# Hand-overs between layers: where the first paired weight tile is summed and split, and when the third plain tile is split

## The chip, the cores and the metric

The kernel runs on one core of a Trainium2 chip. Time is device time in microseconds (us) for one execution, median of three. A profile of one more execution gives the rows shown below. Engine names are those of the profile: PE (TensorE, matrix products; PEld its weight loads), DVE (VectorE), ACT (ScalarE), POOL (GpSimd), SP (SyncE, which here only issues DMAs).

## The reference

Two layers on 512 tokens of width 1024. Each layer is: FFN, mixer, FFN, each one between two RMS norms and added to the residual `h`.

```python
for layer in range(DEPTH):
    g = norm_g[layer]
    f = swiglu_ffn(rms_norm(h, g[0]), ffn_w_gate[layer, 0], ffn_w_up[layer, 0], ffn_w_down[layer, 0])
    h = h + 0.5 * rms_norm(f, g[1])
    hn = rms_norm(h, g[2])
    # layer 0: m = pooling and state-space mixer of hn; layer 1: m = neighbourhood attention of hn
    h = h + rms_norm(m, g[3])
    f = swiglu_ffn(rms_norm(h, g[4]), ffn_w_gate[layer, 1], ffn_w_up[layer, 1], ffn_w_down[layer, 1])
    h = h + 0.5 * rms_norm(f, g[5])
```

`swiglu_ffn` is `(silu(x @ w_gate) * (x @ w_up)) @ w_down` with inner width 2816, so 22 column tiles of 128.

## The kernel before

**Precision.** Every fp32 matrix product is made of three fp32r products: both operands are split into a part `hi` and a rest `lo`, and `mm3` (L170 to L172) adds hi·hi, lo·hi and hi·lo. So each weight tile has to be split before PE can use it: `Weights.hi` copies it on ACT (L113, tile `w_hi`), `Weights.lo` subtracts on DVE or POOL (L124, tile `w_lo`). Activations are transposed on PE (L297) into PSUM (`ps_t`) and evacuated from there in two steps: `xT_hi` on ACT (L318) and `xT_lo` on DVE (L319).

**Paired weight tiles.** An FFN multiplies some column tiles plainly (14 in the first FFN, 2 in the others; gate and up each, so 4 plain weight tiles at the start of the others) and the rest in pairs, by seven products of sums in place of eight. For a pair two raw tiles are loaded, `w_raw` and `w_u`. `Weights.sums` (L95, L96, L98) forms their sums, and the four tiles g, s, u, h that follow are split like plain ones. The sums of the activation blocks are made once for each FFN by `x_sums`: t1, t2, t3, then t4, each split into `xsum..._0` (ACT, L485) and `xsum..._1` (DVE, L488). `x_sums` is a generator; the FFN takes a step of it after each of the four plain tiles of token pair 1.

**A hand-over** is the stretch from the last products of one block to the first of the next. There are five: first FFN to mixer (order "mix"), mixer to FFN, FFN to FFN across the layers, and attention to FFN (order "nat", three of them), and FFN to attention (order "att"). `finish_rows` runs it: products of token tiles 0 and 1, then 2, then 3 (`ps_B`); beside the last of them `residual` adds the normed result to `h` for pair 0, `h_sumsq` (ACT, tile `junk`) and `pre_norm` make `xn`, and `pending()` is `to_xT`: 16 transposes, then 8 evacuations. `first_proj` of the next block multiplies the first four weight tiles with pair 0 (96 products of 256 columns), calls the second `pending()` for pair 1, and multiplies the same four tiles with pair 1.

**What sets the order.** All instructions are issued in the order of the code, to each engine's own queue; an engine waits at its front instruction. On ACT the third next weight tile's `hi` stands ahead of the last sum of squares over `ps_B` and of all evacuations of pair 0:

```python
        W.hi()
        W.hi()
        fg()
        fg = self.post_tile(3, 1, psB, True)
        fg()
        W.lo(nc.gpsimd)
        W.load_ahead()
        W.lo(nc.gpsimd)
        W.load_ahead()
        pending()
```

At most two raw tiles are held at a time, so a load is issued when a `lo` has read an older one. `w_u`, `w_s` lie in the pool `fast`, which `start()` allocates at the beginning of the FFN, after the second `pending()`.

Of the kernel before, what the change touches and what calls it, by code (L numbers as in the profile page):

```python
# [12 lines left out]
ALU = mybir.AluOpType  # L13
# [149 lines left out]
class Builder:  # L163
# [234 lines left out]
        sl = slice(t * P, (t + 1) * P)  # L398
        self.mm3(ps, [x[:, sl] for x in lhs(kt)], [x[:, j * HALF:(j + 1) * HALF] for x in w], start, stop)

    def finish_rows(self, cp, psB, tail, kts, lhs, opened, nxt):


        nc = self.nc
        self.W.fill(self.W.n_split)
        n = 2 * len(tail)

        def product(i, t):
            w = tail[i // 2]
            self.rows(psB[t], lhs, kts[i], t, w, i % 2, not opened and i == 0, i == n - 1)  # L410

        def finish(ts, parts=1):
            for t, sl in self.residual(ts, parts):
                if nxt is None:
                    nc.sync.dma_start(self.out[t * P:(t + 1) * P, sl], self.h[:, t, sl])
            if nxt is not None:
                return self.h_sumsq(cp, ts[0] // 2)

        for i in range(n):
            for t in (0, 1):  # L420
                product(i, t)
        self.post_pair(0, 1, psB)
        s = finish((0, 1))
        for i in range(n):
            product(i, 2)
        fg = self.post_tile(2, 1, psB, True)
        if nxt is None:
            fg()
            finish((2,))
        for i in range(n):  # L430
            product(i, 3)
            if i % 2:
                self.W.done(fill=False)
        if nxt is None:
            self.post_tile(3, 1, psB)
            return finish((3,), 2)

        W = self.W
        W.hi()
        pending = self.pre_norm(cp, 0, s, nxt[0], nxt[1])  # L440
        W.lo()
        W.load_ahead()
        W.hi()
        W.hi()
        fg()
        fg = self.post_tile(3, 1, psB, True)
        fg()
        W.lo(nc.gpsimd)
        W.load_ahead()
        W.lo(nc.gpsimd)  # L450
        W.load_ahead()
        pending()
        return self.pre_norm(cp, 1, finish((2, 3)), nxt[0], nxt[1])


    b_order = list(range(NF))
# [10 lines left out]
    def x_sums(self, forms, tmp, gain=None):  # L467

        nc, tt, W = self.nc, self.nc.vector.tensor_tensor, self.W
        f32 = lambda k, n: [x.bitcast(F32) for x in self.x_block(k, n)]
        b12, b22, t2, t3, t1 = tmp

        def second(out, k):
            if gain is None:
                tt(out=out, in0=f32(k, 1)[0], in1=f32(k, 1)[1], op=ALU.add)
                return
            for kt in range(4 * k, 4 * k + 4):  # L480
                nc.scalar.activation(out=out[:, kt % 4], in_=self.ps_t[kt // 2][:, kt % 2 * 256:(kt % 2 + 1) * 256],
                                     func=AF.Copy, scale=self.gcol[:, gain * KT + kt:gain * KT + kt + 1])

        def hi(n, x):
            nc.scalar.copy(forms[n][0], x)  # L485

        def lo(n, x):
            tt(out=forms[n][1], in0=x, in1=forms[n][0].bitcast(F32), op=ALU.subtract)  # L488

        W.load_ahead()  # L490
        second(b12, 0)
        W.hi()
        second(b22, 1)
        W.sums(W.tiles[W.split][1], nc.vector)
        tt(out=t1, in0=b12, in1=f32(0, 0)[0], op=ALU.subtract)
        tt(out=t1, in0=t1, in1=f32(0, 0)[1], op=ALU.subtract)
        tt(out=t2, in0=t1, in1=b22, op=ALU.subtract)
        tt(out=t3, in0=b22, in1=b12, op=ALU.subtract)
        W.lo()
        W.load_ahead()  # L500
        yield
        W.hi()
        hi(2, t2)
        hi(3, t3)
        hi(1, t1)
        lo(2, t2)
        W.lo()
        lo(3, t3)
        lo(1, t1)
        yield  # L510
        W.hi()
        W.lo()
        t4 = b12
        tt(out=t4, in0=t2, in1=f32(1, 0)[0], op=ALU.add)
        tt(out=t4, in0=t4, in1=f32(1, 0)[1], op=ALU.add)
        yield
        hi(4, t4)
        W.hi()
        lo(4, t4)
        W.lo()  # L520
        W.load_ahead()
        yield
# [5 lines left out]
    def ffn(self, layer, which, gain, nxt, before, ssm=None):  # L528
# [5 lines left out]
        tc, nc, V = self.tc, self.nc, self.nc.vector  # L534
# [4 lines left out]
        def start():  # L539

            z["up"] = tc.alloc_tile_pool(name="up", bufs=1)
            self.W.fast = tc.alloc_tile_pool(name="fast", bufs=1)
            z["t"] = t_pool = tc.alloc_tile_pool(name="xsum", bufs=1, side="right", reuse_waits="tile")
            z["forms"] = forms = {n: [t_pool.tile([P, 4, 256], F32R, name="xsum%d_%d" % (n, i)) for i in range(2)]
                                  for n in (2, 3, 1, 4)}
            tmp = [z["g"][1][:, NF - 6 + 2 * i:NF - 4 + 2 * i].rearrange("p a (b c) -> p (a b) c", c=256)
                   for i in range(3)]
            tmp += [z["up"].tile([P, 1024], F32, tag="m", bufs=2, name="m").rearrange("p (a c) -> p a c", c=256)
                    for _ in range(2)]
            z["sums"] = self.x_sums(forms, tmp, None if ssm else gain)  # L550
            next(z["sums"], None)

        def finish(f, ps_g, ps_u):
            g = z["g"][1][:, f]
            nc.scalar.activation(out=g, in_=ps_g, func=AF.Silu)
            V.tensor_tensor(out=g, in0=g, in1=ps_u, op=ALU.mult)
# [44 lines left out]
        def last_sums(f, up, m, m34):  # L601
            V.tensor_tensor(out=m[:, 256:768], in0=m[:, 256:768], in1=m34, op=ALU.add)  # L602
            if up:
                nc.gpsimd.tensor_tensor(out=rows(f), in0=rows(f), in1=m, op=ALU.mult)  # L604
            else:
                nc.scalar.activation(out=rows(f), in_=m, func=AF.Silu)

        for f in range(n_plain, NF, 2):
            for up in range(2):
# [24 lines left out]
                self.W.done(fill=not last)  # L634
                if not last:
                    last_sums(f, up, m, m34)
        self.W.fast.release()
        self.W.fast = None
        t_pool.release()
        if ssm:  # L640
            self.new_psum(("ps_A", "ps_t"), ("ps_B", "ps_m", "ps_k", "ps_p"))
            self.xT_pool.release()
# [1 line left out]
        r_pools = {n: tc.alloc_tile_pool(name="gT%d" % n, bufs=1, side="right", reuse_waits="tile")  # L644
                   for n in ((8, 2) if ssm else (2, 8))}
        parts, ahead = {}, []
# [12 lines left out]
        order = self.b_order  # L659
# [14 lines left out]
        if ssm:  # L674
            free_pool = tc.alloc_tile_pool(name="free", bufs=1, side="right", reuse_waits="tile")
            free = [free_pool.tile([P, n], F32, name="free%d" % i) for i, n in enumerate((4608, 4608, 2048))]
# [16 lines left out]
        psB = [self.bank("ps_B") for _ in range(TT)]  # L693
        n_out = NF - NTAIL
        tail = []
# [18 lines left out]
        cp = tc.alloc_tile_pool(name="chain", bufs=1)  # L714
        self.chain_begin(cp, 0.5)
        for pair in range(2):
            self.post_pair(pair, 0, psA)
        pending = self.finish_rows(cp, psB, tail, order[n_out:], parts.get, True, nxt)
        return pending, lambda: [p.release() for p in (cp, *list(r_pools.values())[::-1])]

# [1071 lines left out]
```

## Time and profile before

| what | value |
|---|---|
| median of three runs | 1927.48 us (1927.22 to 1929.05) |
| the profiled execution | 1925.91 us, its span 1924.1 us |
| PE busy | 1847.0 us, 96% of the span |
| DVE busy | 1471.0 us, 76% |
| ACT busy | 924.7 us, 48% |
| POOL busy | 349.2 us, 18% |

The span goes from the first to the last instruction; 1.8 us of the profiled execution lie outside it. Busy shares are means over very different stages. Times in rows are counted from the start of the span.

### The profile page before, as it was taken

Reading aid. Unit: us, or ns where it says so; the run is one execution under the profiler, and the core shown is the slowest. Engines: PE = TensorE matmul, PEld = TensorE weight load, DVE = VectorE, ACT = ScalarE, POOL = GpSimd, SP = SyncE. Lnnn points to the kernel's source line nnn. Section 1 sums busy time; section 2 is a strip of 40 time slices with the busy share of each in tenths; the row PEclk is TensorE's granted clock in tenths of the full one; section 3 lists DMA queues with packets and bytes.
Section 4 is the critical chain, followed back from the end, with each engine's and each line's share of the span. In section 5 each row is a group of like instructions: output and inputs, shape, how many; then the busy total and the mean of one; then the engine's idle time right before and its main releaser. Section 6 shows DMA issues by size and latency. Waiting matters only on the chain.

```text
span 1924.1 us, 31539 instructions
## 1 busy us (share of the span) xinstructions
PE 1847.0 (96%) x12368; PEld 1653.5 (86%) x12368; DVE 1471.0 (76%) x2380; ACT 924.7 (48%) x1749; POOL 349.2 (18%) x238
## 2 busy tenths in 40 slices
PE   7999998998899999999899999989999999999998
PEld 7877986887679999988899998879878789999886
DVE  6788979968769999844799996455565569999744
ACT  5244446454455444534545445346555455445432
POOL 1021221014001223100022320001222001332100
PEclk9999999999999999999999999999999999999999
DMA  5464346537422333322233223213222122323321
GB/s 192 144 210 153 110 139 197 194 117 253 157 88 99 108 101 104 116 100 75 78 110 110 99 88 132 99 66 117 93 99 99 66 89 88 111 99 110 114 95 66
DMA packets 82021, 225.48 MB, mean 117 GB/s; under 512 B 15792, under 2 KB 20048, under 8 KB 80848
## 3 DMA queue, kind: packets, MB, share of 16 engines
q1 hardware_dynamic: 70176, 197.80, 30.2%
q0 software_dynamic: 6960, 23.57, 4.1%
q10 hardware_dynamic: 4736, 2.10, 0.4%
q8 instruction: 97, 1.59, 0.3%
q14 instruction: 52, 0.43, 0.1%
HBM read 206.69 MB, written 18.84 MB: 117 GB/s over the span
## 4 chain that ended last, share of the span: by engine, by line
PE 63%; DVE 7%; ACT 2%; DMA 1%; issue 1%; DVEq 0%; ACTq 0%
PE ps_gu L172 10%; PE ps_gu L171 10%; PE ps_gu L170 10%; PE ps_A L172 3%; PE ps_A L171 3%; PE ps_A L170 3%; PE ps_B L172 3%; PE ps_B L171 3%; PE ps_B L170 3%; PE ps_f L170 3%; PE ps_f L171 2%; PE ps_f L172 2%; DVE w_lo L124 1%; PE ps_p L171 1%; PE ps_p L172 1%
## 5 line engine op out<-in xcount | busy, mean ns | idle before, releaser
L124 DVE TENSOR_TENSOR w_lo<-w_raw,w_hi 128x1024 fp32r<-128x1024 f32 x214 | 282.9, 1327 | 212.0 <-ACT w_hi L113 211.9
L113 ACT CAST w_hi<-w_raw 128x1024 fp32r<-128x1024 f32 (+1 forms) x313 | 262.8, 864 | 276.0 <-PE ps_A L172 72.4
L170 PE MATMUL ps_gu<-xsum,w_hi 128*128 128x256 f32 x1088 | 309.0, 284 | 5.7 <-ACT xsum L485 5.7
L171 PE MATMUL ps_gu<-xsum,w_hi 128*128 128x256 f32 x1088 | 309.5, 284 | 2.8 <-DVE xsum L488 2.6
L172 PE MATMUL ps_gu<-xT_hi,w_lo 128*128 128x256 f32 (+1 forms) x1008 | 308.6, 306 | 2.7 <-DVE w_lo L124 2.7
L172 PE MATMUL ps_gu<-xsum,w_lo 128*128 128x256 f32 x1088 | 309.1, 284 | 0.0
L170 PE MATMUL ps_gu<-xT_hi,w_hi 128*128 128x256 f32 (+1 forms) x1008 | 306.6, 304 | 0.0
L171 PE MATMUL ps_gu<-xT_lo,w_hi 128*128 128x256 f32 (+1 forms) x1008 | 306.2, 304 | 0.0
L170 PEld LDWEIGHTS ps_gu<-xsum,w_hi 128*128 128x128 f32 x1088 | 209.3, 192 | 6.3 <-ACT xsum L485 6.3
L171 PEld LDWEIGHTS ps_gu<-xsum,w_hi 128*128 128x128 f32 x1088 | 209.5, 193 | 3.6 <-DVE xsum L488 3.6
L172 PEld LDWEIGHTS ps_gu<-xsum,w_lo 128*128 128x128 f32 x1088 | 209.8, 193 | 0.0
L172 PEld LDWEIGHTS ps_gu<-xT_hi,w_lo 128*128 128x128 f32 x1008 | 191.6, 190 | 14.7 <-DVE w_lo L124 3.7
L170 PEld LDWEIGHTS ps_gu<-xT_hi,w_hi 128*128 128x128 f32 x1008 | 191.7, 190 | 9.0 <-issue 0.7
L171 PEld LDWEIGHTS ps_gu<-xT_lo,w_hi 128*128 128x128 f32 x1008 | 191.4, 190 | 7.5
L98 POOL TENSOR_TENSOR w_u<-w_raw,w_s 128x512 f32<-128x512 f32 x64 | 111.5, 1743 | 381.3 <-ACT w_hi L113 196.1
L124 POOL TENSOR_TENSOR w_lo<-w_raw,w_hi 128x1024 fp32r<-128x1024 f32 x31 | 73.7, 2380 | 569.2 <-ACT w_hi L113 500.6
L113 ACT CAST w_hi<-w_s 128x512 fp32r<-128x512 f32 x136 | 77.7, 621 | 193.7 <-DVE w_s L96 191.6
L96 DVE TENSOR_TENSOR w_s<-w_raw,w_u 128x1024 f32<-128x1024 f32 x68 | 145.8, 2145 | 2.4
L170 PE MATMUL ps_p<-xT_hi,w_hi 128*128 128x256 f32 (+1 forms) x416 | 127.2, 306 | 20.0 <-ACT xT_hi L318 19.7
L172 PE MATMUL ps_A<-w_hi,gT 128*128 128x512 f32 x352 | 138.5, 394 | 6.9 <-DVE gT L657 6.9
L604 POOL TENSOR_TENSOR g<-g,m 128x1024 f32<-128x1024 f32 x34 | 94.6, 2781 | 245.4 <-DVE m L602 239.1
L170 PE MATMUL ps_A<-w_hi,gT 128*128 128x512 f32 x352 | 138.1, 392 | 0.0
(376 smaller groups left out, 4286.2 us busy)
## 6 DMA issues: line engine op xcount, KB each, us to landing
w_raw<-in_w_gu_dram SPq DMA_DIRECT2D x106, 512.0 KB, 3.3
w_raw<-in_w_dn_dram SPq DMA_DIRECT2D x88, 512.0 KB, 3.2
w_u<-in_w_gu_dram SPq DMA_DIRECT2D x70, 512.0 KB, 3.7
w_raw<-in_w_qk_dram SPq DMA_DIRECT2D x16, 512.0 KB, 3.3
bias<-in_att_bias_dram SPq DMA_DIRECT2D x16, 512.0 KB, 4.1
w_raw<-in_w_in_dram SPq DMA_DIRECT2D x8, 512.0 KB, 3.2
cm<-m_dram SPq DMA_DIRECT2D x4, 1024.0 KB, 8.3
w_raw<-in_w_ao_dram SPq DMA_DIRECT2D x8, 512.0 KB, 4.0
```

Source lines behind the costliest of these rows:

```text
L96: tt(out=blocks(s), in0=g[:, :HALF].unsqueeze(1).broadcast_to([P, 2, HALF]), in1=blocks(u)[:, :2], op=ALU.subtract)
L98: (h_engine or self.nc.gpsimd).tensor_tensor(out=u[:, :HALF], in0=g[:, HALF:], in1=s[:, HALF:], op=ALU.add)
L113: self.nc.scalar.copy(hi[:, k:k + step], src[:, k:k + step])
L124: (engine or self.lo_engine).tensor_tensor(out=lo[:, :n], in0=src, in1=hi[:, :n].bitcast(F32), op=ALU.subtract)
L170: mm(ps, a[0], b[0], start=start, stop=False)
L171: mm(ps, a[0], b[1], start=False, stop=False)
L172: mm(ps, a[1], b[0], start=False, stop=stop)
L604: nc.gpsimd.tensor_tensor(out=rows(f), in0=rows(f), in1=m, op=ALU.mult)
```

## The change

Three things are rearranged; no operation is added or taken away.

1. In all five hand-overs the third next plain tile's `hi` and `lo` move from ahead of `pending()` into it, behind the first four of its eight evacuations (`between`).
2. In the three "nat" hand-overs the pool `fast` is allocated in `finish_rows`, on the right side of the memory instead of the left, so that the first `w_u` is loaded there. `hi` of the first paired tile (g) follows the first `pending()`; its `sums` and its `lo` follow `pre_norm` of pair 1, so they stand on DVE ahead of the evacuations of pair 1. In `x_sums` these steps are left out (`gain is None` only for the first FFN).
3. In `x_sums` t4 is computed one step earlier, ahead of the split of t1.

To make room, the pools of the down-projection's input (`gT`) are released inside `finish_rows`, after the last products.

```diff
+        free()
         if nxt is None:
             self.post_tile(3, 1, psB)
             return finish((3,), 2)
...
         W.lo()
         W.load_ahead()
         W.hi()
-        W.hi()
         fg()
         fg = self.post_tile(3, 1, psB, True)
         fg()
         W.lo(nc.gpsimd)
         W.load_ahead()
-        W.lo(nc.gpsimd)
-        W.load_ahead()
-        pending()
-        return self.pre_norm(cp, 1, finish((2, 3)), nxt[0], nxt[1])
+
+        def between():
+            W.hi()
+            W.lo(nc.gpsimd)
+            W.load_ahead()
+
+        ahead = nxt[1] == "nat"
+        if ahead:
+            W.fast = self.tc.alloc_tile_pool(name="fast", bufs=1, side="right")
+            W.load_ahead()
+        pending(between)
+        if ahead:
+            W.hi()
+        pending = self.pre_norm(cp, 1, finish((2, 3)), nxt[0], nxt[1])
+        if ahead:
+            W.sums(W.tiles[W.split][1], nc.vector)
+            W.lo()
+            W.load_ahead()
+        return pending
...
         second(b12, 0)
-        W.hi()
+        if gain is None:
+            W.hi()
         second(b22, 1)
-        W.sums(W.tiles[W.split][1], nc.vector)
+        if gain is None:
+            W.sums(W.tiles[W.split][1], nc.vector)
...
-        W.lo()
-        W.load_ahead()
+        if gain is None:
+            W.lo()
+            W.load_ahead()
         yield
...
         lo(3, t3)
+        t4 = b12
+        tt(out=t4, in0=t2, in1=f32(1, 0)[0], op=ALU.add)
+        tt(out=t4, in0=t4, in1=f32(1, 0)[1], op=ALU.add)
         lo(1, t1)
         yield
         W.hi()
         W.lo()
-        t4 = b12
-        tt(out=t4, in0=t2, in1=f32(1, 0)[0], op=ALU.add)
-        tt(out=t4, in0=t4, in1=f32(1, 0)[1], op=ALU.add)
```

ACT at the hand-over from the mixer to its FFN, before, from `xn` of pair 0 on. `junk,ss_5281` is the last sum of squares over `ps_B`, `junk,ss_h` those of pair 1, and the rows `g<-ps_t` are blocks that `x_sums` reads.

```order
L286 ACTIVATE xn<-h,rs_r 128x512 x2
L113 CAST w_hi<-w_raw 128x1024 x2
L226 ACTIVATE junk,ss_5281<-ps_B 128x512
L318 ACTIVATE xT_hi<-ps_t,gcol 128x256 x8
L226 ACTIVATE junk,ss_h<-h 128x1024 x2
L286 ACTIVATE xn<-h,rs_r 128x512 x2
L318 ACTIVATE xT_hi<-ps_t,gcol 128x256 x8
L481 ACTIVATE g<-ps_t,gcol 128x256 x4
L113 CAST w_hi<-w_raw 128x512 x2
L481 ACTIVATE g<-ps_t,gcol 128x256 x4
L113 CAST w_hi<-w_s 128x512 x2
```

The same place on ACT in the changed kernel:

```order
L286 ACTIVATE xn<-h,rs_r 128x512 x2
L113 CAST w_hi<-w_raw 128x1024
L226 ACTIVATE junk,ss_5281<-ps_B 128x512
L318 ACTIVATE xT_hi<-ps_t,gcol 128x256 x4
L113 CAST w_hi<-w_raw 128x1024
L318 ACTIVATE xT_hi<-ps_t,gcol 128x256 x4
L113 CAST w_hi<-w_raw 128x512 x2
L226 ACTIVATE junk,ss_h<-h 128x1024 x2
L286 ACTIVATE xn<-h,rs_r 128x512 x2
L318 ACTIVATE xT_hi<-ps_t,gcol 128x256 x8
L498 ACTIVATE g<-ps_t,gcol 128x256 x8
L113 CAST w_hi<-w_s 128x512 x2
```

One `w_hi` of 1024 columns has moved behind four evacuations, and the two halves of the paired tile's `w_hi` ahead of the sums of squares of pair 1.

DVE at the same hand-over, before, from `xn` of pair 1 on; L95, L96 and L98 are the weight sums, L495 to L498 give t1, t2 and t3.

```order
L287 TENSOR_SCALAR xn<-h,rs_r 128x512 x2
L319 SCALAR_TENSOR_TENSOR xT_lo<-ps_t,gcol,xT_hi 128x256 x8
L95 TENSOR_TENSOR w_u<-w_u 128x512
L96 TENSOR_TENSOR w_s<-w_raw,w_u 128x1024
L98 TENSOR_TENSOR w_u<-w_raw,w_s 128x512
L495 TENSOR_TENSOR m<-g,xT_hi 128x1024
L496 TENSOR_TENSOR m<-m,xT_lo 128x1024
L497 TENSOR_TENSOR g<-m,g 128x1024
L498 TENSOR_TENSOR m<-g 128x1024
L124 TENSOR_TENSOR w_lo<-w_raw,w_hi 128x1024
L488 TENSOR_TENSOR xsum_1_5585<-g,xsum_0_5584 128x1024
L124 TENSOR_TENSOR w_lo<-w_s,w_hi 128x1024
```

The same place on DVE in the changed kernel:

```order
L287 TENSOR_SCALAR xn<-h,rs_r 128x512 x2
L95 TENSOR_TENSOR w_u<-w_u 128x512
L96 TENSOR_TENSOR w_s<-w_raw,w_u 128x1024
L98 TENSOR_TENSOR w_u<-w_raw,w_s 128x512
L124 TENSOR_TENSOR w_lo<-w_raw,w_hi 128x1024
L319 SCALAR_TENSOR_TENSOR xT_lo<-ps_t,gcol,xT_hi 128x256 x8
L514 TENSOR_TENSOR m<-g,xT_hi 128x1024
L515 TENSOR_TENSOR m<-m,xT_lo 128x1024
L516 TENSOR_TENSOR g<-m,g 128x1024
L517 TENSOR_TENSOR m<-g 128x1024
L505 TENSOR_TENSOR xsum_1_5602<-g,xsum_0_5601 128x1024
L124 TENSOR_TENSOR w_lo<-w_s,w_hi 128x1024
```

Four DVE instructions, the three sums and the split of g, stand between `xn` and the evacuations of pair 1 now.

SP's queue at this hand-over, before; `gpost` is the gain of the next norm, `w_raw` and `w_u` the raw tiles.

```order
L74 DMA w_raw<-in_w_gu_dram 128x1024 x5
L222 DMA gpost<-in_norm_g_dram 128x1024
L71 DMA w_u<-in_w_gu_dram 128x2x512
L74 DMA w_raw<-in_w_gu_dram 128x1024
L71 DMA w_u<-in_w_gu_dram 128x2x512
L74 DMA w_raw<-in_w_gu_dram 128x1024
```

And in the changed kernel:

```order
L74 DMA w_raw<-in_w_gu_dram 128x1024 x5
L71 DMA w_u<-in_w_gu_dram 128x2x512
L74 DMA w_raw<-in_w_gu_dram 128x1024
L71 DMA w_u<-in_w_gu_dram 128x2x512
L74 DMA w_raw<-in_w_gu_dram 128x1024
L222 DMA gpost<-in_norm_g_dram 128x1024
```

Two `w_u` and two `w_raw` loads stand ahead of `gpost` now; before, the first `w_u` also had to wait for the transposes of pair 1, whose input lay in its place.

## Rows read from the trace of the kernel before

**Rows 1.** Waits of PE, whole span: us in total, times, longest us.
```profile
PE ps_p L170 <- ACT xT_hi L318: 19.7, 6, 5.0
...
PE ps_gu L170 <- ACT xsum L485: 5.7, 3, 2.0
```

**Rows 2.** Timeline of ACT, mixer to FFN: start us, us, then the instruction.
```profile
560.18 1.04 ACT L113 CAST w_hi<-w_raw 128x1024 fp32r<-128x1024 f32 x1 [2.96 <-DMA w_raw<-in_w_gu_dram]
561.13 0.59 ACT L226 ACTIVATE junk<-ps_B 128x512 bf16<-128x512 f32 x1
...
561.71 0.83 ACT L318 ACTIVATE xT_hi<-ps_t,gcol 128x256 fp32r<-128x256 f32 x2
562.96 1.60 ACT L318 ACTIVATE xT_hi<-ps_t,gcol 128x256 fp32r<-128x256 f32 x4 [0.42 <-DVE xT_lo L319]
```

**Rows 3.** Timeline of PE, mixer to FFN.
```profile
556.98 1.91 PE L297 MATMUL ps_t<-ident,xn 128*128 128x128 f32 x16
...
589.55 0.28 PE L170 MATMUL ps_gu<-xT_hi,w_hi 128*128 128x256 f32 x1
...
604.88 0.28 PE L170 MATMUL ps_gu<-xT_hi,w_hi 128*128 128x256 f32 x1
```

**Rows 4.** Timeline of DVE, mixer to FFN.
```profile
573.52 0.89 DVE L287 TENSOR_SCALAR xn<-h,rs_r 128x512 f32<-128x512 f32 x2
576.89 2.73 DVE L319 SCALAR_TENSOR_TENSOR xT_lo<-ps_t,gcol,xT_hi 128x256 fp32r<-128x256 f32 x6 [2.48 <-ACT xT_hi L318]
...
581.54 0.69 DVE L95 TENSOR_TENSOR w_u<-w_u 128x512 f32<-128x512 f32 x1 [0.90 <-DMA w_u<-in_w_gu_dram]
...
584.14 1.22 DVE L495 TENSOR_TENSOR m<-g,xT_hi 128x1024 f32<-128x1024 f32 x1
...
589.00 1.22 DVE L124 TENSOR_TENSOR w_lo<-w_raw,w_hi 128x1024 fp32r<-128x1024 f32 x1
```

**Rows 5.** Windows: us, PE busy (instructions), granted PE clock, DMA share, GB/s.
```profile
563.00:565.00 2.00, 2.00 (x9) 0.50 0.66 233
565.00:567.00 2.00, 2.00 (x15) 0.71 0.11 37
...
575.00:577.00 2.00, 2.00 (x20) 1.00 0.00 0
...
600.00:602.00 2.00, 1.26 (x6) 0.58 0.00 0
```

**Rows 6.** Timelines of DVE and PE, FFN to FFN.
```profile
933.36 0.88 DVE L287 TENSOR_SCALAR xn<-h,rs_r 128x512 f32<-128x512 f32 x2
937.60 2.73 DVE L319 SCALAR_TENSOR_TENSOR xT_lo<-ps_t,gcol,xT_hi 128x256 fp32r<-128x256 f32 x6 [3.35 <-ACT xT_hi L318]
...
950.27 0.28 PE L170 MATMUL ps_gu<-xT_hi,w_hi 128*128 128x256 f32 x1
...
953.11 0.28 PE L170 MATMUL ps_gu<-xsum,w_hi 128*128 128x256 f32 x1
...
963.29 0.28 PE L170 MATMUL ps_gu<-xT_hi,w_hi 128*128 128x256 f32 x1
```

**Rows 7.** Timelines of DVE and PE, attention to FFN.
```profile
1571.89 0.88 DVE L287 TENSOR_SCALAR xn<-h,rs_r 128x512 f32<-128x512 f32 x2
1576.04 3.75 DVE L319 SCALAR_TENSOR_TENSOR xT_lo<-ps_t,gcol,xT_hi 128x256 fp32r<-128x256 f32 x8 [3.27 <-ACT xT_hi L318]
...
1604.64 0.28 PE L170 MATMUL ps_gu<-xT_hi,w_hi 128*128 128x256 f32 x1
```

**Rows 8.** Timeline of ACT, FFN to mixer, then FFN to attention.
```profile
415.68 1.34 ACT L286 ACTIVATE xn<-h,rs_r 128x512 f32<-128x512 f32 x2 [1.89 <-DVE rs_r L217]
418.80 2.66 ACT L318 ACTIVATE xT_hi<-ps_t,gcol 128x256 fp32r<-128x256 f32 x6 [1.79 <-PE ps_t L297]
...
1294.39 1.34 ACT L286 ACTIVATE xn<-h,rs_r 128x512 f32<-128x512 f32 x2 [1.88 <-DVE rs_r L217]
1298.59 2.67 ACT L318 ACTIVATE xT_hi<-ps_t,gcol 128x256 fp32r<-128x256 f32 x6 [2.85 <-PE ps_t L297]
```

More of the change, by code (lines that the diff above doesn't have):

```diff
@@ L399, in rows, with finish_rows @@
         self.mm3(ps, [x[:, sl] for x in lhs(kt)], [x[:, j * HALF:(j + 1) * HALF] for x in w], start, stop)
-    def finish_rows(self, cp, psB, tail, kts, lhs, opened, nxt):
+    def finish_rows(self, cp, psB, tail, kts, lhs, opened, nxt, free=lambda: None):
         nc = self.nc
@@ L541, in start @@
             z["up"] = tc.alloc_tile_pool(name="up", bufs=1)
-            self.W.fast = tc.alloc_tile_pool(name="fast", bufs=1)
+            if ssm:
+                self.W.fast = tc.alloc_tile_pool(name="fast", bufs=1)
             z["t"] = t_pool = tc.alloc_tile_pool(name="xsum", bufs=1, side="right", reuse_waits="tile")
@@ L636, in ffn @@
                     last_sums(f, up, m, m34)
+        t_pool.release()
         self.W.fast.release()
         self.W.fast = None
-        t_pool.release()
         if ssm:
@@ L717, in ffn @@
             self.post_pair(pair, 0, psA)
-        pending = self.finish_rows(cp, psB, tail, order[n_out:], parts.get, True, nxt)
-        return pending, lambda: [p.release() for p in (cp, *list(r_pools.values())[::-1])]
+        pending = self.finish_rows(cp, psB, tail, order[n_out:], parts.get, True, nxt,
+                                   lambda: [p.release() for p in list(r_pools.values())[::-1]])
+        return pending, cp.release
     KEY0 = (0, 64, 192, 320)
```

## The prediction

> **What bounds the kernel now.** PE is busy for 1847.0 of 1924.1 us, so I read first what it waits for. The list of PE's waits has two lines that belong to the hand-overs [rows 1]: 19.7 us behind `xT_hi` of ACT, in six places of up to 5.0 us, and 5.7 us behind the activation sums `xsum`, in three places of up to 2.0 us. Next I read one hand-over, mixer to FFN, engine by engine. On ACT the third plain tile's `w_hi` stands 2.96 us idle for its DMA, runs from 560.18, and only then come the last `junk` (0.59 us) and the evacuations, the first at 561.71 [rows 2]. PE had begun the 16 transposes at 556.98 and needs 1.91 us for them [rows 3], so from 558.89 until about 562.5 it has nothing: the evacuations are held up by a weight tile that they don't need. The windows show a second loss: with PE busy again the granted clock is 0.50 from 563 to 565 and 0.71 from 565 to 567, the lower level (1.2 GHz) for most of that time [rows 5]. Half of 2 us and 0.29 of 2 us make 1.6 us of lost work for one such fall. On DVE pair 1's `xn` comes at 573.52, its first `xT_lo` (called S below) at 576.89 and then, after a wait of 0.90 us for `w_u`, the paired tile's sums and the activation sums [rows 4]. PE ends pair 1 at 589.55 = S + 12.66 and the seven products of the pair at 604.88 = S + 27.99 [rows 3]; in FFN to FFN these are 950.27 and 963.29, S + 12.67 and S + 25.69 [rows 6], and attention to FFN ends at S + 28.60 [rows 7]. The pair is 84 products. At full speed 24 of them take 953.11 - 950.27 = 2.84 us [rows 6], 0.1183 each, so 84 take 9.94; the rest, 3.1 to 6.0 us, is waiting and a slow clock behind it (0.58 from 600 to 602 [rows 5]).
>
> **Part 1, the third `w_hi` behind four evacuations.** Its DMA still lands at 560.18, so it still ends at about 561.2, and its `lo` on POOL is not later than before. What changes is what follows it on ACT. Before: `junk`, two evacuations (561.71 to 562.96, with 0.42 idle), two more (half of 1.60), and so the fifth at 561.13 + 0.58 + 1.25 + 0.80 = 563.76 [rows 2]. After: the fifth at 561.13. `junk` and four evacuations fit in the idle 2.96 us: they are 2.63 us with their own idle. The eighth evacuation, and with it pair 1's residual, its sums of squares and `xn`, which follow each other on DVE and ACT without PE, come **2.63 us** earlier in each of the five hand-overs. The first gap of PE shrinks from 3.6 us to some tenths, and with it goes the cause of the fall at 563. PE then does its 96 products of pair 0 in 11.36 us and is ready before `xn` is.
>
> What that is worth depends on what PE waits for next, pair 1's transposes and first evacuation. In the mixer and attention orders nothing new stands in between. The first evacuation comes after half of `xn` (0.67 of 1.34 us), four transposes (a quarter of 1.91, 0.48) and the way between engines, which no row isolates. It is bounded by 0 and by the 0.42 of ACT's idle behind a DVE evacuation [rows 2]; I take 0.30, nearer the row. Sum 1.45 behind `xn`. Before, it came at 418.80 with `xn` at 415.68, and at 1298.59 with `xn` at 1294.39, because PE was late (ACT waits 1.79 and 2.85 for the transposes) [rows 8]. After: 415.68 - 2.63 + 1.45 = 414.50 and 1294.39 - 2.63 + 1.45 = 1293.21. **Gains 4.30 and 5.38.** Work behind it is the same and PE is its limit, so they stay.
>
> **Part 2, the paired tile's work beside the second transposes.** In the three nat hand-overs DVE now has, between `xn` and the first `xT_lo`, its three sums (581.54 to 584.14, 2.60) and one `w_lo` (1.22) [rows 4]. With 0.89 of `xn` ahead, S comes at 573.52 - 2.63 + 0.89 + 2.60 + 1.22 = 575.60, against 576.89: 1.29 earlier. FFN to FFN: 933.36 + 2.08 = 935.44 against 937.60 [rows 6], 2.16 earlier; attention to FFN: 1571.89 + 2.08 = 1573.97 against 1576.04 [rows 7], 2.07 earlier. So most of what part 1 brings here goes into a **new wait**: transposes start with the end of `xn`, at about 571.8, end at 573.7, and PE stands until 576.1 for the first `xT_lo`, 2.4 us. ACT's evacuations of pair 1 stand behind the same DVE, as each waits for the one before to be taken over. What the sums need must be there: `w_u` is now loaded to a place of its own, which waits for no transposes of pair 1 and can be issued when the third plain tile's raw data land, at 560.18; ACT's whole wait for such a tile is 2.96 us [rows 2], so I put its landing at about 563, some 9 us ahead of DVE. The paired raw tile is loaded when POOL has read an older one, which no row times; it too has until pair 1's sums of squares, and its `w_hi` needs 1.04 us [rows 2] on ACT, which has nothing else between the eighth evacuation and those sums. The DMA of `gpost`, now behind four weight loads on SP, is used a norm later; it costs nothing.
>
> In return DVE is free behind the evacuations. From S it needs 8 `xT_lo` (3.75 [rows 7]), four activation sums (4 x 1.22), then in turn split t2, `lo` of s, split t3, two operations of t4, split t1, `lo` of u, split t4 and `lo` of h (each 1.22): t4 is split at S + 18.4 and h at S + 19.6. PE gets to the pair at S + 12.67 and to its last twelve products, those of t4 and h, six forms of 1.42 us later, at S + 21.2. Nothing waits, so the pair ends at S + 12.67 + 9.94 = S + 22.61. **Gains behind S: 27.99 - 22.61 = 5.38, 25.69 - 22.61 = 3.08, 28.60 - 22.61 = 5.99.** If that cover of 1.6 to 2.8 us is gone, each us of DVE or ACT beyond it is lost again.
>
> **Part 3, t4 a step earlier.** It is part of the DVE order just counted. In the first FFN it stands alone; t4 comes up to one split (1.22) sooner. Between 0 and 1.2; no row here shows that PE waits there, so 0.
>
> **The sum.** Mixer and attention orders 4.30 + 5.38 = 9.68. Nat: 1.29 + 5.38 = 6.67, 2.16 + 3.08 = 5.24, 2.07 + 5.99 = 8.06, together 19.97. In all 29.65 of 1925.91. Against it stands the unknown cost of the new waits: PE waits about a us for `xn`, works 1.9 us on transposes, waits 2.4 us. Does the clock fall there? Waits of 3.6 brought a fall [rows 5], and those behind `xsum` of at most 2.0 [rows 1] brought one at 600 [rows 5]; transposes and products without a wait at 575 to 577 kept 1.00 [rows 5]. So 0 to 1.6 in each of three places, 0 to 4.8. The rows are on both sides, and I take half, 2.4. That leaves 27.25: 1898.7 for an execution like the profiled one. The median of the three is 1.57 above that execution, so **1900.2 us**.
>
> The Trainium skill speaks against the change here: "TensorE: Matmul & The Clock Gate", section "HAM oscillation — how this bites in real kernels", says that pauses of PE between bursts of products put the clock back, so that each burst starts slow. By it each new wait would cost a fall, the gain would be 24.85 (29.65 - 4.8) and not 27.25; by the row at 575 alone, 29.65. The row at 600 agrees with the page for a short wait, but no row here shows a wait, transposes and a wait in turn.
>
> **The rivals.** *The new DVE work eats the gain of nat.* If all three falls happen and pairs still wait behind ACT's splits, say half of the 14.45 us behind S is lost (7.2): 29.65 - 4.8 - 7.2 = 17.6, or 14 to 24 with either less or more. For it: four instructions are put ahead of evacuations for which PE then stands, and ACT's order was worked out above only for `w_hi` of g. Against: DVE's order leaves t4 2.8 us. Time 1909.9, from 1903.5 to 1913.5. *More than forecast.* No fall, and part 3 and a shorter way between engines bring what I took as 0: 29.65 + 1.2 + up to 1.5: over 32 only with both, below 1895.5. *It does not do what it says.* The fifth evacuation could be held by something other than the tile, such as PSUM or DVE, so that `xn` does not move, and sums ahead of `xT_lo` then cost 4.7 - 3.37 = 1.3 us a place, about what `xsum` gives back: 1927. Against it: `xT_lo` takes 0.47 each and keeps up with 0.40 of ACT. *Slower.* `w_u` or the paired raw tile lands late. DVE's first sum then stands at the head of its queue with all evacuations of pair 1 behind it, and late `w_hi` of g holds pair 1's sums of squares on ACT. Each us beyond the end of `xn` at about 571.8 (`w_u`), or beyond ACT's arrival at those sums of squares (g's raw tile), is lost on PE whole, in three places. The sum is turned at 9.9 us late in each; at 12 us it is slower by 6.3, 1933.8. For it: before, DVE did wait for `w_u` (0.90 at 581.54 [rows 4]). Against: there its place had been occupied, and the windows around show queues that are not full (share 0.66, then 0.11 and 0.00 [rows 5]).
>
> **How the numbers follow.** About 0.2% (3.9 us) is what a measurement of this kernel tells from no change. Chances: forecast, gain 24 to 32, 0.62; eaten in nat 0.25; more 0.06; not as it says 0.03; slower 0.04. The range holds the forecast with its bounds (1895.5 to 1903.5) and reaches below by 2 us into the rival of more gain, and above into that of nat, to a gain of 18, so that about 2 in 10 are left out: 1893.5 to 1909.5. Faster 0.93 (the first three), same 0.03, slower 0.04.
>
> **What would show it.** Right: in the profile after, ACT's third `w_hi` still begins at about 560.2 with four evacuations ahead of it and the fifth right behind; PE's waits behind `xT_hi` in the first halves are gone and granted clock there is 1.00; `xn` of pair 1 is 2.6 us earlier from the same start; PE waits 2 to 2.5 us for `xT_lo` of pair 1 in nat; no wait behind `xsum`; the pair ends at S + 22.6. Wrong: a granted clock of 0.5 behind that new wait, a DMA as the releaser of the first weight sum or of g's `w_hi`, or a wait on DVE's or ACT's splits in the pair.

## The result and the profile after

The changed kernel takes 1897.45 us (median of four runs, 1895.58 to 1900.18) against 1927.35 us of the kernel before: 29.9 us less, ratio 0.985 with a 95% interval of 0.9839 to 0.9862. The forecast was 1900.2 us, the range 1893.5 to 1909.5. Two executions of all those told of here lie far outside, one of the kernel before (2244.45 us) and one with t4 back (8118.72 us), at granted clocks of 0.75 and 0.20 and for no reason that the record shows; the ratios leave them out, and without its own the kernel with t4 back (e3) has a median of 1901.19 us and not 1902.67. The profiled execution of the changed kernel has a span of 1896.3 us (before 1924.1). PE is busy for 1834.5 us, less than before, though it does the same products: the stretches at the low clock are fewer (mean granted clock 0.994 against 0.984).

PE's waits over the whole span, changed kernel (us in total, times, longest), to compare with [rows 1]:

```profile
PE ps_p L171 <- DVE xT_lo L319: 7.4, 6, 2.2
...
PE ps_p L170 <- ACT xT_hi L318: 1.9, 1, 1.9
...
PE ps_gu L171 <- DVE xsum L505: 0.3, 2, 0.2
```

The 19.7 us behind `xT_hi` have become 1.9, the 5.7 behind `xsum` 0.3, and the 1.2 behind `xT_lo`, with a longest of 0.4, are 7.4 now, with a longest of 2.2. Now the hand-over from mixer to FFN, ACT's timeline first, then PE's and DVE's, to compare with [rows 2 to 4]:

```profile
558.23 1.05 ACT L113 CAST w_hi<-w_raw 128x1024 fp32r<-128x1024 f32 x1 [0.24 <-DMA w_raw<-in_w_gu_dram]
559.18 0.83 ACT L318 ACTIVATE xT_hi<-ps_t,gcol 128x256 fp32r<-128x256 f32 x2
```

```profile
555.03 1.91 PE L297 MATMUL ps_t<-ident,xn 128*128 128x128 f32 x16
...
569.85 1.97 PE L297 MATMUL ps_t<-ident,xn 128*128 128x128 f32 x16 [0.92 <-ACT xn L286]
574.13 0.39 PE L171 MATMUL ps_p<-xT_lo,w_hi 128*128 128x256 f32 x1 [2.19 <-DVE xT_lo L319]
...
586.22 0.28 PE L170 MATMUL ps_gu<-xT_hi,w_hi 128*128 128x256 f32 x1
...
596.23 0.28 PE L170 MATMUL ps_gu<-xT_hi,w_hi 128*128 128x256 f32 x1
```

```profile
569.08 0.88 DVE L287 TENSOR_SCALAR xn<-h,rs_r 128x512 f32<-128x512 f32 x2
...
573.60 0.87 DVE L319 SCALAR_TENSOR_TENSOR xT_lo<-ps_t,gcol,xT_hi 128x256 fp32r<-128x256 f32 x2
...
591.29 1.22 DVE L505 TENSOR_TENSOR xsum<-g,xsum 128x1024 fp32r<-128x1024 f32 x1
```

The tile's DMA still ends ACT's wait, but only 0.24 us are left of 2.96, and the fifth evacuation follows directly. PE has two new waits, 0.92 us ahead of the second transposes and 2.19 us behind them. The pair takes 596.23 - 586.22 = 10.01 us, where it took 15.33 [rows 3].

The start of a hand-over has moved by what came before it, so I count each from its first transposes. Those of the kernel before that [rows 3] does not show, and the end of pair 1 in the last nat hand-over (PE's timeline):

```profile
398.79 1.91 PE L297 MATMUL ps_t<-ident,xn 128*128 128x128 f32 x16
916.42 1.91 PE L297 MATMUL ps_t<-ident,xn 128*128 128x128 f32 x16
1276.16 1.91 PE L297 MATMUL ps_t<-ident,xn 128*128 128x128 f32 x16
1555.32 1.91 PE L297 MATMUL ps_t<-ident,xn 128*128 128x128 f32 x16
1588.71 0.28 PE L170 MATMUL ps_gu<-xT_hi,w_hi 128*128 128x256 f32 x1
```

The changed kernel's, PE, and the first evacuation of pair 1 on ACT in the mixer and attention orders:

```profile
400.57 1.91 PE L297 MATMUL ps_t<-ident,xn 128*128 128x128 f32 x16
908.24 1.91 PE L297 MATMUL ps_t<-ident,xn 128*128 128x128 f32 x16
940.56 0.28 PE L170 MATMUL ps_gu<-xT_hi,w_hi 128*128 128x256 f32 x1
950.56 0.28 PE L170 MATMUL ps_gu<-xT_hi,w_hi 128*128 128x256 f32 x1
1261.81 1.91 PE L297 MATMUL ps_t<-ident,xn 128*128 128x128 f32 x16
1534.59 1.91 PE L297 MATMUL ps_t<-ident,xn 128*128 128x128 f32 x16
1565.88 0.28 PE L170 MATMUL ps_gu<-xT_hi,w_hi 128*128 128x256 f32 x1
1575.89 0.28 PE L170 MATMUL ps_gu<-xT_hi,w_hi 128*128 128x256 f32 x1
```

```profile
416.39 1.94 ACT L318 ACTIVATE xT_hi<-ps_t,gcol 128x256 fp32r<-128x256 f32 x4
...
1277.98 2.67 ACT L318 ACTIVATE xT_hi<-ps_t,gcol 128x256 fp32r<-128x256 f32 x6
```

With [rows 3], [rows 6 to 8] of before that gives, in us:

| term | forecast gain | measured | from |
|---|---|---|---|
| mixer order, to the first evacuation | 4.30 | 4.19 | 20.01 to 15.82 |
| attention order, to the first evacuation | 5.38 | 6.26 | 22.43 to 16.17 |
| mixer to FFN, to the end of pair 1 | 1.29 | 1.38 | 32.57 to 31.19 |
| its pair | 5.38 | 5.32 | 15.33 to 10.01 |
| FFN to FFN, to the end of pair 1 | 2.16 | 1.53 | 33.85 to 32.32 |
| its pair | 3.08 | 3.02 | 13.02 to 10.00 |
| attention to FFN, to the end of pair 1 | 2.07 | 2.10 | 33.39 to 31.29 |
| its pair | 5.99 | 5.92 | 15.93 to 10.01 |
| sum | 29.65 | 29.72 | |

The two profiled spans differ by 27.8, since this execution came 1.78 us late to the first hand-over (400.57 against 398.79); the stretches between the hand-overs differ by -1.6 to +1.0 us, 0.1 in all. The medians differ by 29.9.

The granted clock of the changed kernel in windows (us, PE busy, clock, DMA share, GB/s), behind the first transposes of mixer to FFN and then behind the new wait of the three nat hand-overs:

```profile
559.00:563.00 4.00, 4.00 (x34) 1.00 0.79 265
...
575.00:577.00 2.00, 1.98 (x15) 1.00 0.91 358
...
929.00:931.00 2.00, 2.00 (x11) 0.50 1.00 397
...
1555.00:1557.00 2.00, 1.99 (x15) 1.00 1.02 403
```

The fall at the first evacuations is gone. Of the three new waits one, in FFN to FFN, had 0.50 behind it, and there the stage gained 0.6 us less than forecast.

### The profile page after: what moved, and what is told of

Read it like the earlier page. It is cut to its first block, busy times and chain, and to the rows that moved or that the text cites. A ratio compares the mean times of both kernels' runs of the same rounds, so it can differ in the third digit from the quotient of the medians.

```text
span 1896.3 us, 31539 instructions
## 1 busy us (share of the span) xinstructions
PE 1834.5 (97%) x12368; PEld 1642.3 (87%) x12368; DVE 1471.5 (78%) x2380; ACT 925.5 (49%) x1749; POOL 350.2 (18%) x238
## 4 chain that ended last, share of the span: by engine, by line
PE 65%; DVE 5%; ACT 3%; issue 1%; DMA 1%; DVEq 0%; ACTq 0%
PE ps_gu L172 10%; PE ps_gu L171 10%; PE ps_gu L170 10%; PE ps_A L170 3%; PE ps_A L172 3%; PE ps_A L171 3%; PE ps_B L172 3%; PE ps_B L171 3%; PE ps_B L170 3%; PE ps_f L170 3%; PE ps_f L171 2%; PE ps_f L172 2%; PE ps_qk L884 1%; ACT junk L226 1%; DVE w_lo L124 1%
## 5 line engine op out<-in xcount | busy, mean ns | idle before, releaser
L98 POOL TENSOR_TENSOR w_u<-w_raw,w_s 128x512 f32<-128x512 f32 x64 | 112.2, 1753 | 360.9 <-ACT w_hi L113 196.3
L96 DVE TENSOR_TENSOR w_s<-w_raw,w_u 128x1024 f32<-128x1024 f32 x68 | 145.8, 2144 | 2.4
L171 PE MATMUL ps_A<-w_lo,gT 128*128 128x512 f32 x352 | 137.8, 392 | 0.0
```

The costliest lines, as they stand in the source:

```text
L96: tt(out=blocks(s), in0=g[:, :HALF].unsqueeze(1).broadcast_to([P, 2, HALF]), in1=blocks(u)[:, :2], op=ALU.subtract)
L98: (h_engine or self.nc.gpsimd).tensor_tensor(out=u[:, :HALF], in0=g[:, HALF:], in1=s[:, HALF:], op=ALU.add)
L171: mm(ps, a[0], b[1], start=False, stop=False)
```

## The experiments

My theory was that two mechanisms add up, evacuations freed from a weight tile on ACT and a pair freed from weight work on DVE, and that t4's place does nothing. The rival was that one of the three edits brings most of it.

**Part 1 alone** (e1), on the kernel before:

```diff
-        W.hi()
         fg()
...
-        W.lo(nc.gpsimd)
-        W.load_ahead()
-        pending()
+        def between():
+            W.hi()
+            W.lo(nc.gpsimd)
+            W.load_ahead()
+        pending(between)
```

> Part 1 alone on the kernel before: the third plain tile's hi and lo between the evacuations in all five hand-overs, the pair's work where it was. Theory (the two parts act by themselves; behind S the pair is bound by DVE's order of sums and splits, which starts with S): mixer and attention orders gain what they gain in the changed kernel, 4.25 and 6.26 us by its trace; in each nat hand-over S comes about 3.9 us earlier (2.5 of xn, 1.4 because PE is no longer late for the transposes) and the pair still ends at S + 25.7 to S + 28.6. Gain 10.5 + 3 x 3.9 = 22 us, 1905 us. Rival (the end of the pair hangs on its weight tiles, not on S): PE waits at the pair for as long as S came earlier, nat gains nothing, gain about 10.5, 1917 us.

Measured 1905.56 us against 1926.94, ratio 0.9889 (0.9873 to 0.9904): a gain of 21.4, near the theory's 22. PE's timeline at the pair of mixer to FFN:

```profile
584.22 0.28 PE L170 MATMUL ps_gu<-xT_hi,w_hi 128*128 128x256 f32 x1
...
594.53 0.38 PE L170 MATMUL ps_gu<-xsum,w_hi 128*128 128x256 f32 x1 [2.03 <-ACT xsum L488]
...
600.13 0.28 PE L170 MATMUL ps_gu<-xT_hi,w_hi 128*128 128x256 f32 x1
```

The pair still takes 15.91 us, with the same 2.0 us behind `xsum`: what freed pair 1 did nothing for it. In the three places it takes 15.91, 14.53 and 16.48 us, 0.6 to 1.5 more than before.

**Part 2 with part 3** (e2), the third tile's `hi` back in its old place:

```diff
+        W.hi()
         fg()
...
-        def between():
-            W.hi()
-            W.lo(nc.gpsimd)
-            W.load_ahead()
...
-        pending(between)
+        W.lo(nc.gpsimd)
+        W.load_ahead()
+        pending()
```

> Part 2 (with t4 a step earlier) alone: the pair's sums and split of g ahead of pair 1's evacuations, the third plain tile's hi back ahead of the last junk. Theory: mixer and attention orders gain nothing, PE keeps its 3.3 to 5 us behind xT_hi and the low clock after it in all five; in nat xn does not move, S comes 1.2 us later (xn + 4.5 instead of xn + 3.4), the pair ends at S + 22.6: gain 5.4 + 3.1 + 6.0 - 3.5 = 11 us, 1916.5 us. Rival (part 2 pays only because part 1 made PE early): S later by the full 3.7 us of sums and split, gain 3 us or less, 1924 us or more.

Measured 1914.6 us against 1926.94, ratio 0.9935 (0.9922 to 0.9947): a gain of 12.3, near the theory's 11. The pair takes 10.01 us in its profile. PE keeps 21.1 us behind `xT_hi` in six places:

```profile
PE ps_p L170 <- ACT xT_hi L318: 21.1, 6, 4.8
```

The two gains make 33.7 against 29.9 together. The difference of 3.8 us is about the cover that part 1 takes away: with PE late for the transposes, DVE's four instructions put S off by only 1.2 us (S - `xn` is 3.37 before and 4.53 in e2), and after part 1 by the full 2.5 (1.98 in e1 and 4.52 with both). That is 1.4 us in each of three places, 4.1 in all.

**t4 back** (e3), on the changed kernel, and once more (e10):

```diff
         lo(3, t3)
-        t4 = b12
-        tt(out=t4, in0=t2, in1=f32(1, 0)[0], op=ALU.add)
-        tt(out=t4, in0=t4, in1=f32(1, 0)[1], op=ALU.add)
         lo(1, t1)
         yield
         W.hi()
         W.lo()
+        t4 = b12
+        tt(out=t4, in0=t2, in1=f32(1, 0)[0], op=ALU.add)
+        tt(out=t4, in0=t4, in1=f32(1, 0)[1], op=ALU.add)
         yield
```

> The changed kernel with t4 computed where it was before, behind the split of t1 and of u. Theory (t4's place is not what freed the pair): DVE has the sums of weights off its back, t4's split ends at about S + 19.5 and PE wants it at S + 19.8 to 21.2, so no wait comes back: 1897.5 us as the changed kernel, within 1.5 us. Rival (the wait behind xsum of up to 2.0 us in the kernel before came from t4's place): 1 to 2 us of wait and partly a low clock behind it in each of three places, 1901 to 1906 us.

Measured 1901.19 us, ratio 0.9872 (0.9857 to 0.9889): some 4 us above the changed kernel. I put it down to the clock, since the windows behind the three new waits show 0.51, 0.51 and 0.52 in its profile, and ran the same kernel once more:

> The changed kernel with t4 computed where it was before, once more. The first time it took 1902.67 us, and its profile differed from that of the changed kernel only where the clock was low; between S and the end of the pair both took the same in all three nat hand-overs. Theory (falls of the clock at other waits, not t4's place): this profile has falls at other places than the first, the pairs again end at S + 22.6, and the median is nearer to the changed kernel's 1897, below 1901 us. Rival (t4's place costs 5 us): 1902 us or more, and the same falls as the first time.

Measured 1902.57 us against 1927.95, ratio 0.9874 (0.9859 to 0.9889), and this time 1.00 behind all three waits. My theory falls: the 4 to 5 us (4.6 by the ratios) are there without any fall. Of the rival the time came, and not its falls. DVE in its profile, in the first FFN and in mixer to FFN, and PE from the pair's start to the first products of the next pair:

```profile
191.96 1.23 DVE L505 TENSOR_TENSOR xsum<-g,xsum 128x1024 fp32r<-128x1024 f32 x1 [0.52 <-ACT xsum L502]
...
592.81 1.23 DVE L505 TENSOR_TENSOR xsum<-g,xsum 128x1024 fp32r<-128x1024 f32 x1 [1.17 <-ACT xsum L502]
```

```profile
586.50 0.28 PE L170 MATMUL ps_gu<-xT_hi,w_hi 128*128 128x256 f32 x1
...
596.93 0.28 PE L170 MATMUL ps_gu<-xT_hi,w_hi 128*128 128x256 f32 x1
...
598.03 0.28 PE L171 MATMUL ps_gu<-xT_lo,w_hi 128*128 128x256 f32 x1
```

With t4 made directly ahead of its split, DVE stands 1.17 us until ACT has copied the `hi` part. In the changed kernel two splits lie between, and the row at 591.29 has no wait. Five products into the next pair it is 598.03 - 586.50 = 11.53 us, against 10.49 in the changed kernel (596.71 - 586.22): 1.04 us in each of three places. From S to the same product it is 24.17 us in all three places of e10 and in all three of e3: with t4 back the falls of e3 cost nothing, as DVE was later than PE.

**t4 early alone** (e11), on the kernel before, the same lines moved the other way:

```diff
         lo(3, t3)
+        t4 = b12
+        tt(out=t4, in0=t2, in1=f32(1, 0)[0], op=ALU.add)
+        tt(out=t4, in0=t4, in1=f32(1, 0)[1], op=ALU.add)
         lo(1, t1)
         yield
         W.hi()
         W.lo()
-        t4 = b12
-        tt(out=t4, in0=t2, in1=f32(1, 0)[0], op=ALU.add)
-        tt(out=t4, in0=t4, in1=f32(1, 0)[1], op=ALU.add)
         yield
```

> The kernel before with t4 computed one step earlier and nothing else. Theory (the pair waits in the kernel before because DVE's whole chain of weight sums, activation sums and splits starts with S and has no slack; t4 two operations earlier puts two splits later): PE waits at xsum of t1 or at u instead of t4, S + 25.7 to S + 28.6 stays within 1 us; time within 0.2% of before. Rival (t4's place is what made PE wait for xsum): up to 2 us and a fall of the clock less in each of three places, 5 to 9 us faster.

Measured 1921.71 us against 1927.95, ratio 0.9968 (0.9955 to 0.998): 6.2 us faster, the rival's figure. The pair of mixer to FFN, on PE:

```profile
589.78 0.28 PE L170 MATMUL ps_gu<-xT_hi,w_hi 128*128 128x256 f32 x1
...
603.00 0.28 PE L170 MATMUL ps_gu<-xT_hi,w_hi 128*128 128x256 f32 x1
```

It takes 13.22 us, where it took 15.33; in the other two places it is 1.1 and 2.5 us shorter. PE does wait at other splits now, as the theory said, but for less. So the smallest edit is worth 4 to 6 us in either kernel.

That answers the question of which part brings the gain. Part 1 alone brings 21.4 of 29.9 us, as the rival said. Part 2 without t4, on top of part 1, is worth about 3 us by the ratios (e1 0.9889, then 0.9872 and 0.9874 in e3 and e10, whose intervals overlap that of e1). In e10 the pairs are 4.1 to 6.0 us shorter than in e1, but S comes 2.54 us later behind `xn` in each place, and the stretch from the pair to the next hand-over, or to the end, is 1.5 to 2.5 us longer. Parts 1 and 3 without part 2 were not tried.

**The changed kernel again** (e9), unaltered, measured beside e5, e8 and e7:

> The changed kernel once more, unaltered, beside the next three. In its first profile only one of PE's three new waits of 2.2 us had the low clock behind it, and the kernel with t4 back had it behind all three and was 5 us slower in the median. Theory (which of these waits brings a fall is chance, t4's place does nothing): the profile again has the same waits of 2.2 us, with falls behind other ones than the first time, and falls at other places outside the hand-overs; the median is 1895 to 1902 us. Rival (t4's place keeps the clock up): one fall or none, and the median within 1 us of 1897.5.

Measured 1897.1 us against 1926.67, ratio 0.9851 (0.9837 to 0.9865). The waits are the same, the low clock is behind others: which of them bring it changes between two executions of one program, as the theory said. Its other half, that t4's place does nothing, does not hold after e10. Windows behind the new wait, in the order of the hand-overs:

```profile
574.00:576.00 2.00, 2.00 (x12) 0.50 1.00 406
...
928.00:930.00 2.00, 1.99 (x16) 1.00 0.83 338
1553.00:1555.00 2.00, 2.00 (x9) 0.50 0.68 207
```

The two profiles of one program price a fall. From the first transposes to the end of pair 1 the three stages take 32.05, 31.65 and 31.98 us here, against 31.19, 32.32 and 31.29: with a fall 0.7 to 0.9 us more. And it is given back. PE in mixer to FFN of this run, from the first product after the pair to the next hand-over:

```profile
595.50 0.28 PE L170 MATMUL ps_gu<-xT_hi,w_hi 128*128 128x256 f32 x1
...
906.60 1.91 PE L297 MATMUL ps_t<-ident,xn 128*128 128x128 f32 x16
```

That is 311.10 us; the first profile, with no fall there, needs 908.24 - 596.23 = 312.01. The other two places show the same: 311.25 us with a fall and 311.99 without, 319.74 to the end with a fall and 320.42 without.

**A longer wait** (e5): the split of g done three times over on DVE, so that PE waits longer; the same values are written again.

```diff
...
-        (engine or self.lo_engine).tensor_tensor(out=lo[:, :n], in0=src, in1=hi[:, :n].bitcast(F32), op=ALU.subtract)
+        for _ in range(times):
+            (engine or self.lo_engine).tensor_tensor(out=lo[:, :n], in0=src, in1=hi[:, :n].bitcast(F32), op=ALU.subtract)
...
-            W.lo()
+            W.lo(times=3)
             W.load_ahead()
         return pending
```

> The changed kernel with the split of g done three times on DVE in the three nat hand-overs (the same values written again), so that PE's new wait grows by 2.28 us to about 4.5. Theory (each us that DVE stands between xn and the first xT_lo is lost on PE whole, and a wait this long has the low clock behind it always): S 2.28 us later in three places, 6.8 us, and 0.8 to 1.7 us of slow clock in each place where there was none: 9 to 11 us slower than the changed kernel of the same call. Rival (the pair's products give part of it back, since they wait on something that does not move with S): 3 us or less.

Measured 1905.74 us, ratio 0.9894 (0.9878 to 0.991): 8.6 us above e9, a little under the theory's 9 to 11. The wait behind `xT_lo` grows to a longest of 4.7 us, and the low clock, 0.50, stands behind all three. S comes 2.52 us later behind `xn`, and not the 2.28 expected; three times 2.52 make 7.6 of the 8.6 us.

**A filled wait** (e8): the last four transposes of pair 1 done five times over, the same values, 16 more.

```diff
+        again = self.__dict__.pop("again", 1) if pair == 1 else 1
...
-            for kt in (2 * b, 2 * b + 1):
-                for i in range(by_tile, 2):
-                    transpose(kt, i)
+            for _ in range(again if b == 3 else 1):
+                for kt in (2 * b, 2 * b + 1):
+                    for i in range(by_tile, 2):
+                        transpose(kt, i)
...
+            self.again = 5
         return pending
```

> The changed kernel with the last four transposes of pair 1 done five times over in the three nat hand-overs (the same values, 16 more of 0.12 us), so that PE works through 1.9 of the 2.2 us that it waits. Theory (the low clock behind that wait comes of PE's idleness, and transposes count as work): no fall behind any of the three, S unchanged, up to 2.5 us faster than the changed kernel of the same call if that has three falls, the same if it has none. Rival (the fall comes whatever PE does there, or transposes do not count): falls as before, same time.

Measured 1897.91 us, ratio 0.9854 (0.984 to 0.9868), no faster than e9. Its transposes and the window behind the wait in mixer to FFN (PE's timeline, then windows):

```profile
567.99 3.71 PE L298 MATMUL ps_t<-ident,xn 128*128 128x128 f32 x32 [0.92 <-ACT xn L286]
```

```profile
574.00:576.00 2.00, 1.99 (x16) 1.00 0.92 373
```

The clock is 1.00 behind all three waits, and the time is that of e9, whose profile has two falls. That agrees with e9: what a fall costs here is given back. It does not show that the filling kept the clock up, since e10 had 1.00 behind all three waits with nothing filled.

**The pair on POOL** (e4): sums and split of g moved from DVE to POOL.

```diff
...
         if ahead:
             W.hi()
-        pending = self.pre_norm(cp, 1, finish((2, 3)), nxt[0], nxt[1])
-        if ahead:
-            W.sums(W.tiles[W.split][1], nc.vector)
-            W.lo()
+            W.sums(W.tiles[W.split][1], engine=nc.gpsimd)
+            W.lo(nc.gpsimd)
             W.load_ahead()
-        return pending
+        return self.pre_norm(cp, 1, finish((2, 3)), nxt[0], nxt[1])
```

> The changed kernel with the three sums and the split of g on POOL in the nat hand-overs, so that nothing stands on DVE between xn and the first xT_lo. Theory (PE's new wait behind xT_lo is the cost of those four DVE instructions): the wait of 2.2 us falls to some tenths, S comes about 2.5 us earlier, in three places 7 us, and the fall of the clock that followed one of these waits (0.8 us) goes too: 1890 us. Rival (POOL's slower instructions, about 10 us in all, hold DVE's chain of residual and xn up, or come too late for PE at the pair): no gain or slower, 1897 to 1903 us.

Measured 1908.27 us, ratio 0.9905 (0.9892 to 0.9919): 11 us slower than the changed kernel, worse than the rival. DVE and POOL in its profile:

```profile
563.84 5.60 DVE L266 SCALAR_TENSOR_TENSOR h<-fg,rs_r,h 128x1024 f32<-128x1024 f32 x2
...
570.71 2.17 DVE L280 TENSOR_SCALAR v<-ss_h 128x2 f32<-128x2 f32 x1 [1.27 <-ACT junk L226]
```

```profile
565.09 3.26 POOL L96 TENSOR_TENSOR w_s<-w_raw,w_u 128x1024 f32<-128x1024 f32 x1
...
570.52 2.33 POOL L124 TENSOR_TENSOR w_lo<-w_raw,w_hi 128x1024 fp32r<-128x1024 f32 x1
```

The two residuals take 5.60 us, where the changed kernel's DVE needs 2.48, and an operation on two columns, `v`, takes 2.17 us instead of 0.17: it ends at 572.88, when POOL's split ends (572.85). The first residual ends 1.08 us behind POOL's first sum (566.09 and 565.01), the second 1.08 us behind POOL's second (569.43 and 568.35). PE waits 6.1 us for `xn`. The Trainium skill, "SBUF — State Buffer", section "SBUF: two separate sides", says that DVE and GpSimd share a pair of ports as an exclusive lock held for the whole instruction, and that a DVE instruction with two SBUF inputs, or in a two-port mode, needs it. The rows agree for `h`, which reads `fg` and `h`; `v` reads one tile, and whether it ran in such a mode no row shows.

**The pair in DVE's gaps** (e7): the first sum while ACT makes the sums of squares, only the second ahead of the evacuations, the third and the split of g behind them.

```diff
...
-        pending = self.pre_norm(cp, 1, finish((2, 3)), nxt[0], nxt[1])
+        s = finish((2, 3))
         if ahead:
-            W.sums(W.tiles[W.split][1], nc.vector)
-            W.lo()
-            W.load_ahead()
+            W.sums(W.tiles[W.split][1], nc.vector, (0,))
+        pending = self.pre_norm(cp, 1, s, nxt[0], nxt[1])
+        if ahead:
+            W.sums(W.tiles[W.split][1], nc.vector, (1,))
         return pending
...
+        if gain is not None:
+            W.sums(W.tiles[W.split][1], nc.vector, (2,))
+            W.lo()
         W.load_ahead()
         second(b12, 0)
```

> The changed kernel with the pair's four DVE instructions spread over gaps that DVE has: the first sum while ACT makes pair 1's sums of squares (DVE idles 1.28 us there), only the second ahead of the first xT_lo, the third and the split of g behind the eighth xT_lo, where DVE waits 0.97 us for ACT. Theory (the new wait is the price of those instructions, and DVE's order behind S has about 0.8 us to spare): PE's wait falls from 2.2 to about 0.2 us, S 2.3 us earlier, t4 and h come just in time: 6 to 7 us faster than the changed kernel of the same call, 5 if PE waits a little at the pair's last forms. Rival (DVE is the bound behind S, as in the kernel with part 1 alone): PE waits at the pair instead, gain 1 us or less.

Measured 1891.96 us (1889.86 to 1893.6) against 1926.67, ratio 0.9823 (0.9811 to 0.9836); e9 beside it had 1896.66 to 1897.91. So 5.1 us faster than the changed kernel, at the theory's lower figure. Its DVE and PE:

```profile
566.01 0.88 DVE L291 TENSOR_SCALAR xn<-h,rs_r 128x512 f32<-128x512 f32 x2
...
567.99 2.73 DVE L323 SCALAR_TENSOR_TENSOR xT_lo<-ps_t,gcol,xT_hi 128x256 fp32r<-128x256 f32 x6
```

```profile
580.66 0.28 PE L174 MATMUL ps_gu<-xT_hi,w_hi 128*128 128x256 f32 x1
590.68 0.28 PE L174 MATMUL ps_gu<-xT_hi,w_hi 128*128 128x256 f32 x1
591.27 0.39 PE L176 MATMUL ps_gu<-xT_hi,w_lo 128*128 128x256 f32 x1 [0.19 <-DVE w_lo L128]
```

S comes 1.98 us behind `xn` instead of 4.52, as in e1 where nothing stands between, the pair still takes 10.02, and the next pair's first `w_lo` is now just late.

## Why the prediction was right, and where not

**The sum of the hand-overs stood**, 29.65 forecast and 29.72 measured, term by term within about 0.1 us save two. In FFN to FFN the stage to pair 1's end gained 1.53 for 2.16: the fall of the clock there. In the attention order it gained 6.26 for 5.38: the third raw tile came nearer to the transposes. That these two misses nearly cancel is luck. ACT's third `w_hi` starts 4.90 us behind their start in the profile of before (1281.06 - 1276.16) and 3.89 in the changed one (1265.70 - 1261.81); why it lands sooner was not tried. In e11, where this hand-over is as before, it is 3.73, and in e9, the changed kernel again, 4.54: it moves by about a us from one execution to the next, so some of the 6.26 may be chance. Part 1's own 2.63 was 2.49 (`xn` of pair 1 comes 16.54 us behind the first transposes in the rows of before, and 14.05 after), and `xn` to S took 4.52 for 4.71.

**The step that failed is the cost set against the sum**, 2.4 us for the clock. That half of the waits would bring a fall was near enough: in four profiles with this wait (the changed kernel, e9, e3, e10) it was 1, 2, 3 and 0 of three. But each cost 0.7 to 0.9 us and not the 1.6 taken from the fall at 563, behind a longer wait, and the stretch behind it gave it back (e9, and e8 agrees). Without that term the forecast would have been 1897.8. A granted clock of 0.5 behind the new wait was also named as a sign of being wrong, and it came in one of three places.

The Trainium skill's "TensorE: Matmul & The Clock Gate", section "HAM oscillation — how this bites in real kernels", says that a pause of PE between bursts makes the next burst start slow. The trace agrees in 3 of 3 places with the wait of 4.7 us (e5), and in 6 of 12 with that of 2.2; the section's own example has waits of 3 to 5 us, so that it does not by itself say that each new wait brings a fall, as the prediction read it. The time that would follow from that reading, a gain of 24.85, did not come: what the falls cost was given back behind them.

**Part 3 taken as 0** hid a cause. The prediction has it in DVE's order behind S, but counts that order as if ACT's `hi` copies were always there in time; by that count t4's old place would cost nothing. It costs DVE 1.17 us and PE 1.04 us in each nat place, so that part of what the prediction calls the pairs' gain by part 2 is t4's. Of e10's 5.1 us above the changed kernel the three nat places show 3 x 1.04 = 3.1; the rest is not placed. In the first FFN DVE idles 0.52 us with t4 back, but no row shows what PE loses by it there.

The slack of t4 was wrong as well: it is needed by the sixth of seven forms, at S + 19.8, not by the last, and its split ends at 592.51 = S + 18.9, so there were 0.9 us to spare and not 2.8.

**The rivals.** No DMA was late: neither the first weight sum nor g's `w_hi` waits for one in mixer to FFN. In FFN to FFN g's `w_hi` did wait 0.72 us for its DMA, a sign that the prediction had named; ACT then still waited 1.91 us for the residual, so it cost nothing. The rival that nat gains are eaten did not come, since the pairs run without a wait.

## What to carry to other kernels

When an engine in order stands before a late tile, look at what is queued behind it without needing the tile; here ACT's evacuations waited for a weight, and moving one tile's split behind four of them, in five places, brought 21 us. Price the instructions put ahead of an evacuation, and look for the idle gaps of the same engine first: e7 found three. Make a result that another engine has to touch before you use it some instructions earlier: here two were enough to hide ACT's copy of 1.05 us.

## What the runs showed of the hardware beyond what I had expected

A wait of PE of 2.2 us, 0.9 us of waiting and 16 transposes ahead of it, had the granted clock at 0.50 behind it in 6 of 12 places, in two profiles of one program behind different ones; at 4.7 us it was 3 of 3. POOL instructions held DVE up until they ended, 0.17 us becoming 2.17, while a `w_lo` on POOL beside `xT_lo`, which reads PSUM and one tile, left two of those at 0.88 us.
